# Attention scores from residual rows times query-weighted keys, two heads at once

## The chip, the cores and the metric

The kernel runs on one core of a Trainium2 chip. A core has a TensorE (PE), which multiplies a stationary 128x128 operand by up to 512 moving columns into one PSUM bank, a VectorE (DVE), a ScalarE (ACT), a GpSimd (POOL) and a SyncE (SP), each with its own queue of instructions that it works through in order, and 16 DMA engines that they share. Here SP issues the loads and POOL the stores. The metric is the device time of one execution in microseconds; lower is better.

## The reference

One layer of a streaming encoder on 512 rows of 2048 numbers: four mixers behind one input projection, cross-attention into 256 memory rows with 4 heads of 512, and a feed-forward block, each between two RMS norms. What matters here is the attention, where `h` is the normed residual row and `m` the normed memory:

```python
def memory_cross_attention(h, m, wq, wkv, wo):
    q = (h @ wq).reshape(bsz, T, XA_HEADS, XA_HEAD_DIM)
    k, v = jnp.split(m @ wkv, 2, axis=-1)
    ...
    s = jnp.einsum('bthd,bmhd->bhtm', q, k).astype(jnp.float32) * XA_HEAD_DIM ** -0.5
    p = jax.nn.softmax(s, axis=-1).astype(v.dtype)
    o = jnp.einsum('bhtm,bmhd->bthd', p, v).reshape(bsz, T, D_MODEL)
    return o @ wo
```

All of it is in float32. The output is the residual stream after the three sub-layers.

## The kernel before

**Products.** A float32 operand is split into a high part (rounded to float32r) and a low part, the rest; `split` (L155) makes the high part on ACT and the low part on DVE. `mul3` (L176) adds three products of such parts into a PSUM bank, high by high (L177), high by low (L178) and low by high (L179), so each 128-deep step costs three matmuls. `weights` (L164) loads 256 rows by 512 columns of a weight matrix (512 KB) on SP into `raw` and splits them into `whi` and `wlo`; with `gain` it multiplies each row by a norm's gain on the way (two splits of 512 columns instead of one of 1024). The three names have three buffers each (`wp`). Products go to five PSUM banks called `mm` or three called `ps`.

**Stages around the change.** In phase 1 the keys of each head (`k_d`) and later its values (`v_d`) are computed from the memory and written to DRAM, split. The end of phase 1 is the output projection of the mixers (`y_proj`, with `w_out`), four passes of 512 columns. Behind the last pass `advance` takes each of four blocks of 128 rows through the norm and the residual sum (`ad_x`), transposes the new rows on PE (L231, four banks a block), and splits them into `act`, which holds the residual rows transposed. It also makes the next norm's factor `r2a`; that factor is not multiplied into `act` but into the scores.

In the same stretch `value_out` (L880) runs for heads 0 to 2: it multiplies a head's values by that head's rows of `xa_wo` and writes the product (`vw_d`) to DRAM, 24 matmuls of 512 columns for each of four column passes. Each needs nothing of `advance`, so its matmuls stand between the transposes of `advance` in PE's order.

Phase 2 is a loop over the four heads. `proj_a` multiplies the head's 512 columns of `xa_wq` (with the gain of norm 2) by `act` into four `mm` banks, which are split into `qh` and `ql`. `attention` (L851) loads the head's keys (`at_kh`, `at_kl`) and computes for each block of 128 rows the scores against 256 memory rows in a `ps` bank, then the maximum, the exponential with its row sum, and the division (`at_p`). The probabilities are transposed on PE and split into `pth`, `ptl`, two heads in one pair of tiles. Behind head 0 stands `value_out` for head 3. Then `y_proj` multiplies the probabilities of all heads by `vw_d`.

A scheduler sets the order of each engine's queue from the order of the program and from the buffers; a tile that is asked for while all its buffers are in use makes the instruction that first writes it wait.

## Time and profile before

| What | Value |
|---|---|
| Median of the runs, lowest to highest | 2770.33 us, 2769.64 to 2773.34 |
| The profiled execution's own time | 2771.02 us |
| Its span in the trace | 2769.1 us |
| Granted TensorE clock | 0.989 |
| DMA, mean over the span | 155 GB/s |
| HBM read, written | 351.30 MB, 74.47 MB |
| Loads of `xa_wq` issued | 1077.8 to 1273.5 us, 32 of 512 KB |
| Loads of `xa_wo` issued | 978.7 to 1145.7 us, 32 of 512 KB |

The span is cut into 40 equal slices below; each digit is the busy share of a slice in tenths, 9 meaning 90% or more. A slice is 69.2 us, so the stages above lie in slices 15 to 19 (1003 us is at 14.5 slices, 1308 us at 18.9).

```profile
PE   8999999999999999999979999999999998999997
DVE  5735557446662355434589989888888989999966
ACT  5623423233552245423455545444444445665542
DMA  8732322344675258532654434343333326577656
```

A busy share is a mean over stages with different limits, and matmuls overlap, so the prediction reads stages and starts of instructions.

### The profile page before, as it was taken

The numbers are of one execution on the slowest core, as the hardware profiler recorded it, in microseconds if no ns is written. First come the engines' busy times: TensorE is split into PE (matmuls) and PEld (weight loads), VectorE is DVE, ScalarE is ACT, GpSimd is POOL, SyncE is SP. The second block draws the span as 40 slices with busy tenths as digits, with TensorE's granted clock in tenths as the row PEclk, the third lists the DMA queues.
The fourth block names the chain that finished last, engine by engine and source line by source line (L and its number), as shares of the span: only waits on it lengthen the run. The fifth ranks groups of instructions, "written<-read, shape, count | busy, mean of one in ns | idle before, by whom it ended". The sixth has DMA issues, their size and how long they took to land. (4 is left out here: it accounts for less than half of the span.)

```text
span 2769.1 us, 35279 instructions
## 1 busy us (share of the span) xinstructions
PE 2680.7 (97%) x13426; PEld 2249.7 (81%) x13426; DVE 1942.7 (70%) x2869; ACT 1261.1 (46%) x1918; POOL 139.5 (5%) x219
## 2 busy tenths in 40 slices
PE   8999999999999999999979999999999998999997
PEld 6788788878778877888857888888888887888875
DVE  5735557446662355434589989888888989999966
ACT  5623423233552245423455545444444445665542
POOL 0000000100000001000000000000000000000002
PEclk9999999999999999999989999999999999999998
DMA  8732322344675258532654434343333326577656
GB/s 287 237 105 86 96 69 80 109 130 125 216 256 215 93 188 307 174 100 88 213 185 144 141 118 127 114 130 116 124 122 120 121 103 245 196 198 192 166 125 225
DMA packets 158755, 428.08 MB, mean 155 GB/s; under 512 B 18157, under 2 KB 29306, under 8 KB 147706
## 3 DMA queue, kind: packets, MB, share of 16 engines
q1 hardware_dynamic: 140154, 355.57, 39.2%
q0 software_dynamic: 18432, 70.27, 8.8%
q8 instruction: 105, 1.72, 0.3%
q14 instruction: 64, 0.52, 0.1%
HBM read 351.30 MB, written 74.47 MB: 154 GB/s over the span
## 5 line engine op out<-in xcount | busy, mean ns | idle before, releaser
L162 DVE SCALAR_TENSOR_TENSOR wlo<-raw,PA,whi 128x512 fp32r<-128x512 f32 x368 | 263.1, 747 | 298.7 <-ACT whi L161 298.6
L161 ACT ACTIVATE whi<-raw,PA 128x512 fp32r<-128x512 f32 x368 | 247.8, 718 | 398.0 <-PE mm L178 211.0
L1088 PE MATMUL mm<-L,whi 128*128 128x512 f32 x1448 | 367.8, 396 | 15.7 <-ACT f_x L1111 8.6
L177 PE MATMUL mm<-act,whi 128*128 128x512 f32 x832 | 329.8, 396 | 0.0
L179 PE MATMUL mm<-act,wlo 128*128 128x512 f32 x832 | 326.7, 393 | 0.0
L178 PE MATMUL mm<-act,whi 128*128 128x512 f32 x832 | 326.1, 392 | 0.0
L1088 PEld LDWEIGHTS mm<-L,whi 128*128 128x128 f32 x1448 | 263.4, 191 | 65.0 <-ACT f_x L1111 9.6
L991 ACT CAST whi<-raw 128x1024 fp32r<-128x1024 f32 x176 | 184.9, 1051 | 237.3 <-PE ps L1088 77.3
L177 PE MATMUL mm<-whi,act 128*128 128x512 f32 x640 | 251.6, 394 | 4.2 <-ACT act L158 3.7
L1088 PE MATMUL ps<-L,whi 128*128 128x512 f32 x1016 | 254.8, 392 | 0.0
L178 PE MATMUL mm<-wlo,act 128*128 128x512 f32 x640 | 250.8, 392 | 2.4 <-DVE wlo L162 2.4
L179 PE MATMUL mm<-whi,act 128*128 128x512 f32 x640 | 250.0, 392 | 0.2 <-DVE act L159 0.2
L159 DVE TENSOR_TENSOR wlo<-raw,whi 128x1024 fp32r<-128x1024 f32 x92 | 112.4, 1224 | 191.7 <-ACT whi L158 191.3
L992 DVE TENSOR_TENSOR wlo<-raw,whi 128x1024 fp32r<-128x1024 f32 x176 | 214.0, 1217 | 5.1 <-ACT whi L991 5.1
L1091 PEld LDWEIGHTS mm<-L,wlo 128*128 128x128 f32 x1448 | 198.0, 191 | 18.2 <-DVE wlo L992 4.2
L1088 PEld LDWEIGHTS ps<-L,whi 128*128 128x128 f32 x1016 | 182.6, 189 | 32.6
L1091 PE MATMUL mm<-L,wlo 128*128 128x256 f32 x1448 | 203.3, 283 | 2.7 <-DVE wlo L992 2.7
L991 ACT CAST whi<-sum 128x1024 fp32r<-128x1024 f32 x132 | 137.6, 1045 | 129.3 <-DVE wlo L992 64.6
L992 DVE TENSOR_TENSOR wlo<-sum,whi 128x1024 fp32r<-128x1024 f32 x132 | 161.6, 1224 | 43.4 <-ACT whi L991 42.5
L179 PEld LDWEIGHTS mm<-act,wlo 128*128 128x128 f32 x832 | 156.3, 188 | 32.3 <-issue 0.5
L158 ACT CAST whi<-raw 128x1024 fp32r<-128x1024 f32 x92 | 96.8, 1054 | 186.9 <-PE mm L179 137.6
L178 PEld LDWEIGHTS mm<-act,whi 128*128 128x128 f32 x832 | 156.4, 188 | 30.8 <-issue 0.7
(505 smaller groups left out, 4908.7 us busy)
## 6 DMA issues: line engine op xcount, KB each, us to landing
raw<-in_w_gu_dram SPq DMA_DIRECT2D x186, 512.0 KB, 3.6
raw<-in_w_in_dram SPq DMA_DIRECT2D x88, 512.0 KB, 3.7
rawB<-in_w_down_dram SPq DMA_DIRECT2D x40, 1024.0 KB, 5.0
raw<-in_xa_wkv_dram SPq DMA_DIRECT2D x64, 512.0 KB, 4.4
raw<-in_w_out_dram SPq DMA_DIRECT2D x32, 512.0 KB, 3.9
raw<-in_xa_wo_dram SPq DMA_DIRECT2D x32, 512.0 KB, 6.6
raw<-in_xa_wq_dram SPq DMA_DIRECT2D x32, 512.0 KB, 4.0
raw<-vw_d SPq DMA_DIRECT2D x28, 512.0 KB, 4.2
```

What stands on the lines that cost most here:

```text
L158: nc.scalar.copy(hi, src)
L159: nc.vector.tensor_tensor(lo, src, hi.bitcast(F32), op=ALU.subtract)
L161: nc.scalar.activation(hi, src, AF.Copy, scale=scale)
L162: nc.vector.scalar_tensor_tensor(lo, src, scale, hi.bitcast(F32), op0=ALU.mult, op1=ALU.subtract)
L177: nc.tensor.matmul(o, ah, bh, start=start, stop=False, skip_group_check=reopen)
L178: nc.tensor.matmul(o, ah, bl, start=False, stop=False, skip_group_check=reopen)
L179: nc.tensor.matmul(o, al, bh, start=False, stop=stop, skip_group_check=reopen)
L991: nc.scalar.copy(hl[0], src)
L992: nc.vector.tensor_tensor(hl[1], src, hl[0].bitcast(F32), op=ALU.subtract)
L1088: nc.tensor.matmul(bank, wh[:, k], t[k].rearrange("p s n -> p (s n)"), start=k == 0 and m in (1, 2, 5), stop=k == 7, **kw)
L1091: nc.tensor.matmul(bank[:, 0:256], wl[:, k], t[k][:, 0], start=False, stop=k == 7, **kw)
```

## The change

For each head the query weights are first multiplied by the keys: `g = wq[:, head] @ k[head].T`, 2048 by 256. The scores are then the residual rows times `g`, so the queries themselves are no longer made. The new function `key_query` makes `g` for all four heads, in the place in phase 1 where `value_out` for heads 0 to 2 stood, ahead of those. It reads the transposed query weights (`xa_wqt`, transposed on the host as other weights are laid out there), multiplies by the gain of norm 2 while it splits the product, and writes both parts to DRAM (`g_d`, two heads side by side, 16 MB in all). `attention` now takes a pair of heads: for each of 16 k-steps it multiplies the rows' `act` by 512 columns of `g`, which come from DRAM straight into buffers called `whi` and `wlo`, into four `mm` banks, one for each block of rows. Softmax and transposes are as before, for two heads together. `value_out` for head 3 now stands behind both pairs.

In `key_query` a product's bank has high weights by both key parts in its 512 columns, and low weights by the high keys added to the first 256; the two halves are then added (copy on ACT, add on DVE) and split. The buffers that `g` is split into (`at_vh`, `at_vl`) are those that `value_out` loads values into, two of each.

```diff
+    g_d = dr.tile([2, 2, P, KT, 2 * MEM], F32, name="g_d")
...
+            for h in range(XH):
+                key_query(h, pl)
             for h in range(3):
                 value_out(h, pl, 2)
...
+    def key_query(h, pl):
+        kk = pl.tile([P, 4, 2, MEM], F32R, name="kq_k")
+        for i in range(2):
+            nc.sync.dma_start(kk[:, :, i].bitcast(F32), k_d[h][i].rearrange("p (d m) -> p d m", d=4))
+        for q in range(4):
+            w = [weights(xa_wqt, h * XHD + dc * 2 * P, q * 512) for dc in range(2)]
+            gh, gl = (pl.tile([P, 4 * MEM], F32R, name="at_v" + i, bufs=2).rearrange("p (k m) -> p k m", k=4)
+                      for i in "hl")
+            for j in range(4):
+                js = slice(j * P, (j + 1) * P)
+                o = mm.tile([P, 512], F32, name="mm")
+                for d in range(4):
+                    wh, wl = w[d // 2]
+                    nc.tensor.matmul(o, wh[:, d % 2, js], kk[:, d].rearrange("p s m -> p (s m)"), start=d == 0,
+                                     stop=d == 3, skip_group_check=True)
+                for d in range(4):
+                    nc.tensor.matmul(o[:, 0:MEM], w[d // 2][1][:, d % 2, js], kk[:, d, 0], start=False,
+                                     stop=d == 3, skip_group_check=True)
+                g = pl.tile([P, MEM], F32, name="kq_g", bufs=2)
+                nc.scalar.copy(g, o[:, MEM:])
+                nc.vector.tensor_tensor(g, o[:, 0:MEM], g, op=ALU.add)
+                split(gh[:, j], gl[:, j], g, gcol(2, q * 4 + j))
+            for i, src in enumerate((gh, gl)):
+                nc.gpsimd.dma_start(g_d[h // 2, i, :, 4 * q:4 * q + 4, h % 2 * MEM:(h % 2 + 1) * MEM], src.bitcast(F32))
...
-    def attention(h, qh, ql, pl, ph, pl_):
+    def attention(act, p, pl, ph, pl_):
...
+        o = [mm.tile([P, 512], F32, name="mm") for _ in range(NT)]
+        lhs = act_lhs(act)
+        for kc in range(KT // 2):
+            g = [wp.tile([P, 2, 512], F32R, name=n) for n in ("whi", "wlo")]
+            for i in range(2):
+                nc.sync.dma_start(g[i].bitcast(F32), g_d[p, i, :, 2 * kc:2 * kc + 2])
+            for t in range(NT):
+                for kk in range(2):
+                    k = kc * 2 + kk
+                    ah, al = lhs(k, t)
+                    mul3(o[t], ah, al, g[0][:, kk], g[1][:, kk], k == 0, k == KT - 1)
...
-                for h in range(XH):
-                    qh = pl.tile([P, 4, T], F32R, name="at_qh", bufs=2)
-                    ql = pl.tile([P, 4, T], F32R, name="at_ql", bufs=2)
-                    proj_a(act, xa_wq, h * XHD, lambda j, o: split(qh[:, j], ql[:, j], o), 2)
-                    ks = slice(2 * (h % 2), 2 * (h % 2) + 2)
-                    attention(h, qh, ql, pl, pt[h // 2][0][:, ks], pt[h // 2][1][:, ks])
-                    if h == 0:
-                        value_out(3, pl)
+                for p in range(2):
+                    attention(act, p, pl, *pt[p])
+                value_out(3, pl)
```

Three places in the engines' order show what stands where. First PE beside the transposes of the second row block of `advance` (`ad_x`), before; `mm` are banks, `at_vh` the values of `value_out`:

```order
L177 MATMUL mm_8269<-whi_8272,at_vh_8176 128x512
L231 MATMUL ps_7983<-C_83,ad_x_7963 128x128 x4
L231 MATMUL ps_7991<-C_83,ad_x_7963 128x128 x4
L178 MATMUL mm_8269<-wlo_8273,at_vh_8176 128x512
L231 MATMUL ps_7999<-C_83,ad_x_7963 128x128 x4
```

And the same place now:

```order
L870 MATMUL mm_8380<-kq_k_8177,whi_8326 128x512
L233 MATMUL ps_7984<-C_83,ad_x_7964 128x128 x4
L870 MATMUL mm_8380<-kq_k_8177,whi_8326 128x512
L233 MATMUL ps_7992<-C_83,ad_x_7964 128x128 x4
L233 MATMUL ps_8000<-C_83,ad_x_7964 128x128 x4
L870 MATMUL mm_8380<-kq_k_8177,whi_8332 128x512 x2
L873 MATMUL mm_8380<-kq_k_8177,wlo_8327 128x256 x2
```

`value_out` has gone from between the transposes, and `key_query` has taken its place; up to the last transpose of `advance` there were 142 matmuls of the one, and there are 178 of the other.

Second, SP's queue where the keys of head 2 are loaded, with what each row waits for (a semaphore of PE, of DVE, or of an earlier DMA):

```order
L168 DMA raw_8834<-in_xa_wqt_dram 128x2x512 [waits DMAHW3_49,DMAHW0_49,DVE_49]
L168 DMA raw_8840<-in_xa_wqt_dram 128x2x512 [waits DMAHW1_49,DVE_49]
L860 DMA kq_k_8759<-k_d2_91 128x4x256 [waits PE_49]
L860 DMA kq_k_8759<-k_d2_91 128x4x256
L168 DMA raw_8906<-in_xa_wqt_dram 128x2x512 [waits DMAHW2_49,DVE_49]
L168 DMA raw_8912<-in_xa_wqt_dram 128x2x512 [waits DMAHW3_49,DVE_49]
```

These loads are new; the first of the two waits for PE, and the weight loads behind it for their turn. Further down the same queue, where `value_out` of head 0 begins (`xa_wo` are its weights):

```order
L168 DMA raw_9391<-in_xa_wo_dram 128x2x512 [waits DMAHW7_49,DMAHW4_49,DVE_49]
L168 DMA raw_9409<-in_xa_wo_dram 128x2x512 [waits DMAHW5_49,DMAHW0_49,DVE_49]
L168 DMA raw_9435<-in_xa_wo_dram 128x2x512 [waits DMAHW6_49,DVE_49]
L923 DMA at_vh_9341<-v_d0_93 128x1024 [waits DMASW4_49,DMASW5_49,DMASW2_49,DMASW0_49]
L923 DMA at_vl_9342<-v_d0_93 128x1024 [waits DMASW5_49,DMASW6_49,DMASW3_49,DMASW1_49]
```

Before, the values of heads 0 and 1 were loaded ahead of the output projection; now head 0's follow five of the weight loads, and wait for stores of POOL (DMASW).

Third, DVE in the middle of `key_query` (`kq_g` the product that is added up, `at_vl` its low part, `wlo` the low part of the next weights):

```order
L877 TENSOR_TENSOR kq_g_8885<-mm_8876,kq_g_8885 128x256
L877 TENSOR_TENSOR kq_g_8899<-mm_8890,kq_g_8899 128x256
L161 TENSOR_TENSOR wlo_8981<-raw_8978,whi_8980 128x1024
L164 SCALAR_TENSOR_TENSOR at_vl_8847<-kq_g_8885,PA_84,at_vh_8846 128x256
L164 SCALAR_TENSOR_TENSOR at_vl_8847<-kq_g_8899,PA_84,at_vh_8846 128x256
```

The banks go in pairs, with a split of weights between the steps of a pair; in `value_out` DVE had the split of weights alone.

More of the change, by code (lines that the diff above doesn't have):

```diff
@@ L71, in build @@
           gdn_dt_bias, gdn_norm_g, ssm_conv_w, ssm_conv_b, ssm_A_log, ssm_dt_bias, ssm_D,
-          ssm_norm_g, w_out, xa_wq, xa_wkv, xa_wo, w_gu, w_down, w_last, cst, out, dbg=None,
+          ssm_norm_g, w_out, xa_wqt, xa_wkv, xa_wo, w_gu, w_down, w_last, cst, out, dbg=None,
           phases=(1, 2, 3)):
@@ L94, in build @@
     x, mem = x[0], mem[0]
-    w_in, w_out, xa_wq, xa_wkv, xa_wo = w_in[0], w_out[0], xa_wq[0], xa_wkv[0], xa_wo[0]
+    w_in, w_out, xa_wkv, xa_wo = w_in[0], w_out[0], xa_wkv[0], xa_wo[0]
     pool_w = pool_w[0]
@@ L848, in v_load @@
         return mt
-    def attention(h, qh, ql, pl, ph, pl_):
-        hl = [pl.tile([P, 1024], F32R, name="at_k" + s, bufs=2) for s in "hl"]
-        for s in range(2):
-            nc.sync.dma_start(hl[s].bitcast(F32), k_d[h][s])
-        kh, kl = (a.rearrange("p (d m) -> p d m", d=4) for a in hl)
+    def key_query(h, pl):
[23 more added lines that the diff above has]
+    def attention(act, p, pl, ph, pl_):
         sc = float(XHD) ** -0.5
-        pr = pl.tile([P, NT, MEM], F32, name="at_p")
         rs = sm.tile([P, 2 * NT], F32, name="at_rs")
@@ L861, in attention @@
         nc.vector.tensor_scalar(rs[:, NT:], r2a, -sc, None, op0=ALU.mult)
-        for t in range(NT):
-            ts_ = slice(t * P, (t + 1) * P)
-            s = ps.tile([P, 512], F32, name="ps")[:, :MEM]
-            for d in range(4):
-                mul3(s, qh[:, d, ts_], ql[:, d, ts_], kh[:, d], kl[:, d], d == 0, d == 3)
-            mx = sm.tile([P, 1], F32, name="at_mx")
-            nc.vector.tensor_reduce(mx, s, axis=AX.X, op=ALU.max)
-            nc.vector.tensor_tensor(mx, mx, rs[:, NT + t:NT + t + 1], op=ALU.mult)
-            sum_ = sm.tile([P, 1], F32, name="at_s")
-            nc.scalar.activation(pr[:, t], s, AF.Exp, bias=mx, scale=rs[:, t:t + 1], accum_out=sum_)
+        o = [mm.tile([P, 512], F32, name="mm") for _ in range(NT)]
[9 more added lines that the diff above has]
+                    mul3(o[t], ah, al, g[0][:, kk], g[1][:, kk], k == 0, k == KT - 1)
+        pr = pl.tile([P, NT, 512], F32, name="at_p", bufs=2)
+        for t in range(NT):
+            mx = sm.tile([P, 2], F32, name="at_mx")
+            nc.vector.tensor_reduce(mx, o[t].rearrange("p (h m) -> p h m", h=2), axis=AX.X, op=ALU.max)
+            nc.vector.tensor_scalar(mx, mx, rs[:, NT + t:NT + t + 1], None, op0=ALU.mult)
+            sum_ = sm.tile([P, 2], F32, name="at_s")
+            for i in range(2):
+                ms = slice(i * MEM, (i + 1) * MEM)
+                nc.scalar.activation(pr[:, t, ms], o[t][:, ms], AF.Exp, bias=mx[:, i:i + 1], scale=rs[:, t:t + 1],
+                                     accum_out=sum_[:, i:i + 1])
             nc.vector.reciprocal(sum_, sum_)
-            nc.vector.tensor_scalar(pr[:, t], pr[:, t], sum_, None, op0=ALU.mult)
-        for m in range(2):
+            for i in range(2):
+                ms = slice(i * MEM, (i + 1) * MEM)
+                nc.vector.tensor_scalar(pr[:, t, ms], pr[:, t, ms], sum_[:, i:i + 1], None, op0=ALU.mult)
+        for m in range(4):
             tp = ps.tile([P, T], F32, name="ps")
@@ L1356 @@
         'gdn_dt_bias', 'gdn_norm_g', 'ssm_conv_w', 'ssm_conv_b', 'ssm_A_log', 'ssm_dt_bias', 'ssm_D',
-        'ssm_norm_g', 'w_out', 'xa_wq', 'xa_wkv', 'xa_wo', 'w_gu', 'w_down', 'w_last', 'cst']
+        'ssm_norm_g', 'w_out', 'xa_wqt', 'xa_wkv', 'xa_wo', 'w_gu', 'w_down', 'w_last', 'cst']
 _OUTS = [((1, T, D), 'float32')]
@@ L1364, in laid_out @@
     a['cst'] = constants()
+    a['xa_wqt'] = np.ascontiguousarray(np.asarray(inputs['xa_wq'])[0].T)
     w = np.asarray(inputs['ffn_w_gu'])[0].reshape(2, 8, P, 2, HT, P)
```

## The prediction

> **What bounds the kernel now.** I began with the page's first part, to see which engine is full:
>
> ```profile
> PE 2680.7 (97%) x13426; PEld 2249.7 (81%) x13426; DVE 1942.7 (70%) x2869; ACT 1261.1 (46%) x1918; POOL 139.5 (5%) x219
> ```
>
> TensorE is busy 97% of the span, so a change of matmul counts should show in the time. But a busy share says nothing about one stage, so I asked for the windows of the stages that the change touches: from the end of the first output projection to the last row transposes of `advance` (1003 to 1054 us), the rest of `value_out` for heads 0 to 2 (to 1085), and attention with head 3's `value_out` (to 1308.4). Columns: the window, its length, then busy time of PE, weight loads, DVE, ACT and POOL, TensorE's clock, DMA share, GB/s.
>
> ```profile
> 1003.00:1054.00 51.00, 44.95 (x220) 36.08 (x219) 43.40 (x128) 33.76 (x49) 8.04 (x15) 0.97 0.84 304
> 1054.00:1085.00 31.00, 30.19 (x131) 24.08 (x130) 15.09 (x31) 15.93 (x22) 5.00 (x10) 1.00 0.83 271
> 1085.00:1308.40 223.40, 223.40 (x1076) 187.08 (x1075) 85.13 (x149) 79.61 (x133) 6.33 (x12) 1.00 0.43 140
> sum 305.40, PE 298.54 PEld 247.25 DVE 143.62 ACT 129.29 POOL 19.37; mean PE 99.51 PEld 82.42 DVE 47.87 ACT 43.10 POOL 6.46
> ```
>
> The third window is pure TensorE: no gap, DVE and ACT under 40%, DMA at 0.43. In the first, TensorE already has gaps, DVE is busy 43.4 of 51 us and DMA 0.84. **The change moves work out of the third window, where only TensorE is scarce, into the first, where everything is scarce.** All else stays, so the sum is for these 305.4 us.
>
> Next, the price of one matmul. Matmuls overlap, so I read the timeline of starts, not durations:
>
> ```profile
> 1125.72 0.39 PE L179 MATMUL mm<-act,wlo 128*128 128x512 f32 x1
> ...
> 1129.80 0.39 PE L179 MATMUL mm<-act,wlo 128*128 128x512 f32 x1
> 1130.03 0.28 PE L177 MATMUL ps<-at_kh,at_qh 128*128 128x256 f32 x1
> ...
> 1131.34 0.28 PE L179 MATMUL ps<-at_kh,at_ql 128*128 128x256 f32 x1
> ```
>
> 18 steps in 4.08 us: 0.2267 us for 512 columns. 11 steps in 1.31 us: 0.119 us for 256.
>
> **The change, part by part. Tensor work.** Removed: the query projection, 4 heads x 16 k x 4 columns x 3 = 768 at 0.2267 = 174.1 us, and the scores, 4 x 4 x 4 x 3 = 192 at 0.119 = 22.9; together 197.0. Added: `key_query`, 64 banks x (4 of 512 + 4 of 256 columns) = 256 x 0.2267 + 256 x 0.119 = 88.5, and the new scores, 2 pairs x 16 k x 4 row blocks x 3 = 384 x 0.2267 = 87.1; together 175.6. Were every stage like the third window, the gain would be **21.4 us**. The 32 transposes of the probabilities stay.
>
> **The third window after.** 223.4 - 197.0 + 87.1 = 113.5 us. The weights of these scores come by DMA as they are: two 512 KB loads per 24 matmuls (5.44 us), 193 GB/s, under the 304 of the first window; buffers are three deep, so I cost them at nothing. The softmax of a pair is behind its last matmuls: a reduction and two exponentials of
>
> ```profile
> L868 DVE TENSOR_REDUCE at_mx<-ps 128x1 f32<-128x256 f32 x16 | 6.6, 422 | 3.3 <-PE ps L179 3.1
> L871 ACT ACTIVATE at_p<-ps,at_mx,at_rs 128x256 f32<-128x256 f32 x16 | 9.0, 563 | 14.8 <-DVE at_mx L869 14.8
> ```
>
> 0.56 us each and two scalings, some 3 us. The new order puts matmuls of the fifth bank, and then of `value_out`, between the transposes; I take 1.5 us for each of the two pairs (ends 0 and 3): 116.5.
>
> **`value_out` of heads 0 to 2**, now after all of `key_query`: 288 x 0.2267 = 65.3, its own cover unchanged.
>
> **First stage: `key_query` beside `advance`.** Per block of four banks it asks TensorE for 5.53 us. Its price on DVE, by issue distance:
>
> ```profile
> 1600.61 1.22 DVE L992 TENSOR_TENSOR wlo<-sum,whi 128x1024 fp32r<-128x1024 f32 x1 [0.34 <-ACT whi L991]
> 1601.75 0.42 DVE L1166 TENSOR_TENSOR f_t<-mm,f_t 128x256 f32<-128x256 f32 x1
> 1602.09 1.21 DVE L1037 TENSOR_TENSOR sum<-sum,raw 128x1024 f32<-128x1024 f32 x1
> 1603.22 0.42 DVE L1168 SCALAR_TENSOR_TENSOR f_t<-f_t,f_t 128x256 f32<-128x256 f32 x1
> ```
>
> 1.13 us for a weight's low part, 0.34 for a 256-column add from a bank. The scaled subtraction has a column as its scalar; by
>
> ```profile
> L162 DVE SCALAR_TENSOR_TENSOR wlo<-raw,PA,whi x368: 706/746/754, 8.4 to 1289.0; 128x512 fp32r<-128x512 f32 x184
> L162 DVE SCALAR_TENSOR_TENSOR act<-ps,PB,act x16: 339/346/353, 727.4 to 789.0; 128x128 fp32r<-128x128 f32 x16
> ```
>
> 256 columns take about 0.48 us, 0.40 by issue. A block: 2 x 1.13 + 4 x 0.74 = 5.2 us of DVE if it never waits. But copy (ACT), add (DVE), scaled copy (ACT) and subtraction (DVE) hand over four times per bank with two `kq_g` buffers:
>
> ```profile
> L1165 ACT COPY f_t<-mm 128x256 f32<-128x256 f32 x44 | 16.1, 366 | 10.3 <-PE mm L1091 10.3
> L158 ACT CAST whi<-raw 128x1024 fp32r<-128x1024 f32 x92 | 96.8, 1054 | 186.9 <-PE mm L179 137.6
> ```
>
> With 0.37, 0.42, 0.48 and 0.48 the chain of a pair of banks, overlapped as the order has it, is about 1.9 us; with one weight split beside it 2.9 or so: **5.9 us a block**. Ends: 5.5 (TensorE alone) and 8.1 (the four steps one after the other, 7.0, and a 1.05 us cast).
>
> The steps of `advance` itself, and where the stage ended before (the last of its transposes on PE):
>
> ```profile
> 1020.28 2.74 DVE L765 SCALAR_TENSOR_TENSOR ad_x<-y,rs_r,ad_x 128x512 f32<-128x512 f32 x4
> 1024.01 1.89 DVE L159 TENSOR_TENSOR act<-ps,act 128x512 fp32r<-128x512 f32 x3 [0.99 <-ACT act L158]
> ...
> 1028.53 0.16 DVE L151 TENSOR_TENSOR rsq_t<-nr_r 128x1 f32<-128x1 f32 x1
> 1028.60 0.15 DVE L151 TENSOR_TENSOR rsq_t<-rs_r 128x1 f32<-128x1 f32 x1
> 1028.72 0.16 DVE L152 SCALAR_TENSOR_TENSOR rsq_t<-rsq_t,mr_v 128x1 f32<-128x1 f32 x1
> ```
>
> ```profile
> 1051.19 0.65 PE L231 MATMUL ps<-C,ad_x 128*128 128x128 f32 x4
> ```
>
> Until those transposes the new order has 178 of the 512 `key_query` matmuls. DVE must issue in that time 19 adds (6.5 us), 18 subtractions (7.2), 10 low parts (11.3), 16 row updates at 0.67 (10.7), 16 splits at 0.60 (9.6) and some 80 small steps at 0.09 (7.3): 53 us. The same count before (12 low parts, 13.6, no adds or subtractions, two evictions, 1.2) gives 42.4 in 51.0 us, so 8.6 of waits; with them and 3 more for the new hand-overs **65 us** (ends 53 and 77). TensorE needs 42 of these, so DVE is the bound here.
>
> **The rest of `key_query`: new waits.** `kq_k` has one buffer, so head h+1's keys can be loaded only after head h's last matmul; SP holds that load and the weight loads queued behind it, and TensorE, in order, waits for both halves. What such a pair of 512 KB loads takes:
>
> ```profile
> raw<-in_xa_wq_dram SPq DMA_DIRECT2D x32, 512.0 KB, 4.0
> raw<-in_xa_wo_dram SPq DMA_DIRECT2D x32, 512.0 KB, 6.6
> at_vh<-v_d SPq DMA_DIRECT2D x4, 512.0 KB, 8.9
> at_kh<-k_d SPq DMA_DIRECT2D x4, 512.0 KB, 10.4
> ```
>
> 4.0 with free engines, 10.4 in a burst. The new blocks move 2.1 MB in under 6 us, so the engines are near full: I take 6.5. And a wait of that kind has an aftermath:
>
> ```profile
> 1021.13 1.89 PE L231 MATMUL ps<-C,ad_x 128*128 128x128 f32 x8 [2.90 <-issue]
> 1022.67 0.77 PE L178 MATMUL mm<-wlo,at_vh 128*128 128x512 f32 x1
> ...
> 1024.52 0.45 PE L177 MATMUL mm<-whi,at_vh 128*128 128x512 f32 x1
> ```
>
> After 2.9 us idle matmuls last 0.77 us, not 0.39, until 1024.5, some 1.5 us lost. So 8 us for a head change (ends 4 and 12). The first of the three falls into the stage that DVE bounds anyway (42 + 8 < 65): nothing. Left are 334 matmuls: the rest of head 1, 2.44 blocks x 5.9 = 14.4; heads 2 and 3, each 22.1 + 8, in whose pause DVE and ACT catch up: 60.2. **74.6 us** (ends 58 + 2 x 4 = 66, and 10.4 x 8.1 + 24 = 108).
>
> The Trainium skill, "DMA: Bandwidth & Descriptors", section "Anatomy of one DMA", fits one transfer (for the other issuing path) as about 2.0 us plus bytes over 436e3 per us; a 1.05 MB pair would be 4.4 us by it, an estimate, and the sum 4.2 us shorter. The 8.9 and 10.4 rows speak against it here.
>
> **From `key_query` to `value_out`.** The values used to be loaded far ahead, head 0's at 854.0 us:
>
> ```profile
> L884 SPq DMA_DIRECT2D at_vh<-v_d x4: 442/463/477, 854.0 to 1097.3; - x4
> ```
>
> Now they take the buffers (`at_v`) that the last blocks write to DRAM from, and stand on SP behind five weight loads, the last of which waits for a split that waits for the last block. So they are issued about when TensorE runs dry: the 8.9 us row, **9 us** (ends 4 and 12).
>
> **Sum.** 65 + 74.6 + 9 + 65.3 + 116.5 = 330.4, against 305.4: **25.0 us more**. The profiled execution took 2771.0 us (span 2769.1), 0.7 over the median 2770.3, so 2796.0 there and 2795 as a median. With all ends low 53 + 66 + 4 + 65.3 + 113.5 = 302, 4 us faster; with all high 77 + 108 + 12 + 65.3 + 119.5 = 382, 76 slower.
>
> **Rivals.**
> 1. *The pauses vanish under the evictions* (faster). If the keys land while ACT and DVE still drain the five banks and the split weights, TensorE's pauses cost nothing of their own and DVE's issue time alone counts: 55 + 60.5 + 4 + 65.3 + 113.5 = 298, **2763**. It decides if a pair of key loads lands within some 4 us (five banks at 0.74). For it: the 4.0 us row. Against: 6.6, 8.9 and 10.4. Chance 0.08.
> 2. *Pauses half as long and good overlap*: 57 + 66 + 5 + 65.3 + 114.5 = 308, **2773**, no change to speak of. Chance 0.09.
> 3. *The transfers are the bound*: the two stages move 46 MB (16.8 of weights, 16.8 written, 4.2 of keys, 8.4 of `advance`). At the busiest stretch of before,
>
> ```profile
> 1020.00:1040.00 20.00, 16.54 (x81) 13.52 (x81) 16.36 (x45) 12.65 (x19) 4.29 (x8) 0.91 0.93 334
> 1040.00:1060.00 20.00, 19.33 (x95) 15.70 (x94) 18.37 (x63) 14.42 (x21) 3.22 (x6) 1.00 0.96 352
> ```
>
> that is 131 to 138 us, less than my 140; but the three pauses also hold SP's weight loads, and if these gaps cannot be filled it is 135 + 24 = 159: **2815**. Chance 0.13.
> 4. *The hand-overs do not overlap*: 8.1 us a block. 77 + 10.4 x 8.1 + 16 + 9 + 65.3 + 116.5 = 368, **2833**. For it: two `kq_g` buffers, and splits of weights that stand between the steps. Against: the order issues them in pairs. Chance 0.12.
>
> **How the numbers follow.** My forecast, 2795 with a range of its own of 2779 to 2812, gets 0.58. About 0.2% (5.5 us) is what a measurement can tell from no change. Faster is rival 1, 0.08; within 0.2% rival 2, 0.09; slower the rest, 0.83. The range that leaves out rival 1 and most of rival 4 is 2771 to 2828.
>
> **What would show it.** Right: PE gaps of 5 to 10 us at each change of `kq_k` and before the first `at_vh` matmul, put down to those DMAs; DVE over 85% busy until the last `ad_x` transposes, and these 12 to 16 us later than at 1051; from the first new score on no gap over 2 us and about 192 matmuls in 44 us. Wrong: gaps under 3 us at the head changes (rivals 1, 2); DMA share at 0.95 with PE waiting for `raw` (rival 3); ACT and DVE waiting for each other through all 16 blocks at 8 us (rival 4). A slower clock over the whole kernel, or a loss outside these stages, would make all of it wrong.

## The result and the profile after

The changed kernel takes 2822.4 us (median of 4 runs, 2820.3 to 2823.8), the kernel before 2771.7 beside it: ratio 1.0185, 95% interval 1.0173 to 1.0197. The forecast was 2795: slower, as measured, but the loss is 51 us and not 25. 2822 lies outside the forecast's own range, 2779 to 2812, and inside the wider one, 2771 to 2828.

The page's first part, after: TensorE has 64 matmuls fewer and is busy as long as before, in a span 50.9 us longer.

```profile
PE 2680.5 (95%) x13362; PEld 2246.1 (80%) x13362; DVE 1970.3 (70%) x2921; ACT 1293.2 (46%) x1998; POOL 164.1 (6%) x251
```

From here on "the stretch" is the time from the end of the output projection to the first matmul on the probabilities `pth`: 305.0 us before, 357.7 after in the profiled runs. Outside it little moved: ahead of it 1003.5 us before and 1001.2 after, behind it 1460.6 and 1461.1. The windows of the changed kernel, cut at the prediction's stages (columns as there): to the last row transposes; the rest of head 1; pause, head 2; pause, head 3; the hand-over; `value_out` 0 to 2; a gap; attention with `value_out` 3.

```profile
1001.00:1062.90 61.90, 45.77 (x242) 37.56 (x241) 49.67 (x157) 39.79 (x72) 8.22 (x12) 0.86 0.70 247
1062.90:1085.00 22.10, 16.09 (x81) 13.20 (x79) 18.25 (x48) 14.86 (x28) 4.17 (x6) 0.92 0.83 278
1085.00:1093.00 8.00, 0.00 (x0) 0.01 (x1) 5.30 (x9) 3.90 (x9) 1.85 (x3) 0.66 1.02 327
1093.00:1119.30 26.30, 25.34 (x128) 20.97 (x128) 16.80 (x30) 16.25 (x31) 3.60 (x5) 0.91 0.71 248
1119.30:1127.80 8.50, 0.00 (x0) 0.01 (x1) 5.70 (x10) 4.21 (x10) 2.41 (x4) 0.64 1.02 348
1127.80:1153.50 25.70, 25.03 (x128) 20.73 (x128) 16.80 (x30) 16.19 (x31) 3.55 (x5) 0.92 0.72 251
1153.50:1162.70 9.20, 0.01 (x1) 0.03 (x1) 5.70 (x10) 4.26 (x10) 2.46 (x4) 0.62 0.97 303
1162.70:1237.80 75.10, 69.93 (x288) 56.27 (x288) 25.43 (x21) 33.75 (x43) 11.95 (x22) 0.93 0.83 270
1237.80:1242.40 4.60, 0.16 (x1) 0.00 (x0) 0.00 (x0) 0.00 (x0) 0.00 (x0) 0.86 1.00 361
1242.40:1358.90 116.50, 116.09 (x513) 94.55 (x514) 29.50 (x58) 28.12 (x58) 4.34 (x8) 0.98 0.63 217
```

Four windows hold no matmul but for a stray record, and in each the DMA share is 0.97 or more: TensorE stands while transfers are under way. Who it waited for in this stretch (total, times, longest):

```profile
PE mm L870 <- DMA kq_k<-k_d: 23.0, 3, 8.6
PE mm L179 <- DMA at_vh<-v_d: 9.2, 1, 9.2
PE mm L873 <- DVE wlo L161: 6.8, 3, 4.8
PE mm L870 <- DVE kq_g L877: 4.9, 4, 3.1
PE mm L179 <- DMA whi<-g_d: 4.5, 1, 4.5
```

Each pause has a tail. The timeline of TensorE behind the last of them, where the scores begin:

```profile
1242.42 2.48 PE L179 MATMUL mm<-whi,act 128*128 128x512 f32 x4 [4.45 <-DMA whi<-g_d]
1244.69 0.63 PE L180 MATMUL mm<-wlo,act 128*128 128x512 f32 x1
1245.12 0.63 PE L181 MATMUL mm<-whi,act 128*128 128x512 f32 x1
...
1247.25 0.63 PE L181 MATMUL mm<-whi,act 128*128 128x512 f32 x1
1247.68 0.52 PE L179 MATMUL mm<-whi,act 128*128 128x512 f32 x1
1248.03 0.40 PE L180 MATMUL mm<-wlo,act 128*128 128x512 f32 x1
```

Starts are 0.43 us apart until 1247.7, then 0.23: for 5.3 us after 4.45 us of idleness matmuls go at half rate, some 2.4 us lost. All this against the forecast:

| Stage | Forecast us | Measured us |
|---|---|---|
| to the last `ad_x` transposes | 65 | 61.9 |
| rest of head 1 | 14.4 | 22.1 |
| heads 2 and 3 with their pauses | 60.2 | 68.5 |
| hand-over to `value_out` | 9 | 9.2 |
| `value_out` 0 to 2 | 65.3 | 75.1 |
| first load of `g` | 0 | 4.6 |
| attention and `value_out` 3 | 116.5 | 116.5 |
| sum | 330.4 | 357.9 |

### The profile page after: what moved, and what is told of

Its sections match the earlier page's. It is cut to its first block, busy times and chain, and to the rows that moved or that the text cites. A ratio compares the mean times of both kernels' runs of the same rounds, so it can differ in the third digit from the quotient of the medians.

```text
span 2820.0 us, 35497 instructions
## 1 busy us (share of the span) xinstructions
PE 2680.5 (95%) x13362; PEld 2246.1 (80%) x13362; DVE 1970.3 (70%) x2921; ACT 1293.2 (46%) x1998; POOL 164.1 (6%) x251
## 5 line engine op out<-in xcount | busy, mean ns | idle before, releaser
L164 DVE SCALAR_TENSOR_TENSOR wlo<-raw,PA,whi 128x512 fp32r<-128x512 f32 x304 | 218.0, 748 | 198.7 <-ACT whi L163 198.6
L163 ACT ACTIVATE whi<-raw,PA 128x512 fp32r<-128x512 f32 x304 | 205.4, 720 | 306.5 <-PE mm L180 145.1
L161 DVE TENSOR_TENSOR wlo<-raw,whi 128x1024 fp32r<-128x1024 f32 x124 | 151.2, 1224 | 252.5 <-ACT whi L160 252.4
L179 PE MATMUL mm<-whi,act 128*128 128x512 f32 x768 | 303.1, 396 | 6.6 <-DMA whi<-g_d 4.5
L180 PE MATMUL mm<-wlo,act 128*128 128x512 f32 x768 | 301.5, 393 | 1.8 <-DVE wlo L164 1.8
L181 PE MATMUL mm<-whi,act 128*128 128x512 f32 x768 | 300.8, 393 | 0.2 <-DVE act L161 0.2
L1025 ACT CAST whi<-raw 128x1024 fp32r<-128x1024 f32 x176 | 185.1, 1052 | 237.4 <-PE mm L1122 70.5
L160 ACT CAST whi<-raw 128x1024 fp32r<-128x1024 f32 x124 | 130.4, 1053 | 231.9 <-PE mm L181 183.9
L179 PE MATMUL mm<-act,whi 128*128 128x512 f32 x576 | 230.4, 400 | 0.0
L181 PE MATMUL mm<-act,wlo 128*128 128x512 f32 x576 | 227.7, 395 | 0.0
L180 PE MATMUL mm<-act,whi 128*128 128x512 f32 x576 | 227.0, 394 | 0.0
L1026 DVE TENSOR_TENSOR wlo<-raw,whi 128x1024 fp32r<-128x1024 f32 x176 | 214.3, 1218 | 5.3 <-ACT whi L1025 5.3
L179 PEld LDWEIGHTS mm<-whi,act 128*128 128x128 f32 x768 | 145.2, 189 | 39.2 <-DMA whi<-g_d 4.9
L180 PEld LDWEIGHTS mm<-wlo,act 128*128 128x128 f32 x768 | 145.2, 189 | 32.6 <-DVE wlo L164 3.0
```

The source lines that it names most:

```text
L160: nc.scalar.copy(hi, src)
L161: nc.vector.tensor_tensor(lo, src, hi.bitcast(F32), op=ALU.subtract)
L163: nc.scalar.activation(hi, src, AF.Copy, scale=scale)
L164: nc.vector.scalar_tensor_tensor(lo, src, scale, hi.bitcast(F32), op0=ALU.mult, op1=ALU.subtract)
L179: nc.tensor.matmul(o, ah, bh, start=start, stop=False, skip_group_check=reopen)
L180: nc.tensor.matmul(o, ah, bl, start=False, stop=False, skip_group_check=reopen)
```

## The experiments

**Theory.** The loss is TensorE's waits for loads that cannot be issued before the last reader of their only buffer is done, each with its tail at half clock, and the hand-overs between ACT and DVE. **Rival.** The transfers bind in any order: the change moves 34 MB more (the profiles count 428.1 MB before and 461.7 after). The medians, with the ratio to the kernel before, and the stretch of each profiled run:

| Run | Median us | Ratio, 95% interval | Stretch us |
|---|---|---|---|
| changed kernel | 2822.4 | 1.0185, 1.0173 to 1.0197 | 357.7 |
| changed_again | 2826.9 | 1.0196, 1.0181 to 1.0211 | 363.1 |
| swap | 2830.4 | 1.0213, 1.0198 to 1.0229 | 361.1 |
| two_k | 2813.5 | 1.0150, 1.0135 to 1.0165 | 347.0 |
| own_v | 2818.2 | 1.0168, 1.0147 to 1.0188 | 350.1 |
| two_k_own_v | 2806.4 | 1.0126, 1.0110 to 1.0143 | 339.9 |
| eight_e | 2798.7 | 1.0098, 1.0079 to 1.0117 | 331.7 |
| eight_e_own_g | 2805.8 | 1.0124, 1.0105 to 1.0142 | 344.4 |
| half_stores | 2790.2 | 1.0070, 1.0049 to 1.0091 | 326.5 |
| long_runs | 2798.4 | 1.0098, 1.0081 to 1.0116 | 335.0 |
| four_kq_g | 2791.6 | 1.0072, 1.0056 to 1.0088 | 325.9 |
| vo3_back | 2829.2 | 1.0210, 1.0194 to 1.0226 | 356.0 |
| values_first | 2781.8 | 1.0039, 1.0026 to 1.0052 | 313.0 |
| values_first_half | 2768.2 | 0.9993, 0.9984 to 1.0002 | 305.8 |
| four_raw | 2782.7 | 1.0039, 1.0026 to 1.0052 | 314.7 |
| interleaved | 2798.5 | 1.0094, 1.0079 to 1.0109 | 333.7 |
| interleaved_2 | 2788.5 | 1.0068, 1.0054 to 1.0082 | 322.9 |
| interleaved_3 | 2790.4 | 1.0077, 1.0064 to 1.0090 | 323.5 |

**How far these numbers carry.** Two runs settle it: the changed kernel itself again, and one part undone.

> The changed kernel once more, nothing edited. If the 7 us by which the control and vo3_back were slower come from the edits, this is 2822 again, with the output projection ending at 1001 us. If they come from what differs between one set of runs and the next, ahead of the stretch, this can come out as far as 2829, with a later end of the output projection and the same 358 us from there to the first matmul on the probabilities.

It ran from 2820.2 to 2832.9, with a stretch of 363.1 us and the end of the output projection at 1005.4 instead of 1001.2. Two edits further down that leave the work as it is, vo3_back and swap, gave medians of 2829.2 and 2830.4 and stretches of 356.0 and 361.1. So a difference of up to 8 us between two medians, or 7 us between two single stretches, shows nothing by itself, and I lean on waits that come or go and on differences above that.

```diff
-                for p in range(2):
-                    attention(act, p, pl, *pt[p])
-                value_out(3, pl)
+                attention(act, 0, pl, *pt[0])
+                value_out(3, pl)
+                attention(act, 1, pl, *pt[1])
```

> One part of the change undone: value_out of head 3 stands between the two pairs again, all else as in the changed kernel. The forecast had 116.5 us for attention and value_out 3, and this stretch took that. So no part of the loss should lie here: 2822 within 4 us. Rival (the new place of value_out 3 costs: its weights hold up the next stage, or the softmax of pair 0 was covered better): 3 us or more below 2822.

Measured 2829.2, but a stretch of 356.0: the 7 us are inside the spread of the changed kernel itself. No loss shows in the new place of `value_out` 3.

**Buffers for keys and values.** The pools of this stage leave 2 KB of SBUF, too little for a second `kq_k`. So the pool of `y` was put on top and closed after head 1; first alone, as a control:

```diff
-            yp = pool("yp", stack=s1)
             pl = pool("adp", stack=s1)
+            syp = ExitStack()
+            yp = pool("yp", stack=syp)
...
-            for h in range(XH):
+            for h in range(2):
+                key_query(h, pl)
+            syp.close()
+            for h in range(2, XH):
                 key_query(h, pl)
```

> Control for the next three: the pool of y is put above that of advance and closed after head 1 of key_query, so that its 41 KB can be used again; nothing else is edited, but the loads of ad_x for the next stage may now start earlier. Theory (each loss is a load that must wait for the last reader of its one buffer): the same time as the changed kernel, 2822 within 4 us, the three kq_k waits of 6.4, 8.1 and 8.6 us and the at_vh wait of 9.2 us all still there. Rival (the transfers are the bound): the 2 MB of ad_x that come earlier lengthen the stretch by about 6 us, 2828.

2830.4, stretch 361.1, inside the spread; all four waits are still there (23.7 us in three for `kq_k`, 9.3 for `at_vh`). The 8 us above 2822 are near what the rival had forecast for the early `ad_x`, but the unchanged kernel reached 2833 as well, so neither is decided. Then with a second `kq_k`:

```diff
+            kp = pool("kqp", stack=s1)
             for h in range(2, XH):
-                key_query(h, pl)
+                key_query(h, pl, kp if h == 2 else pl)
...
-        kk = pl.tile([P, 4, 2, MEM], F32R, name="kq_k")
+        kk = kp.tile([P, 4, 2, MEM], F32R, name="kq_k")
```

> As the control, with a second kq_k buffer for head 2, so that the keys of heads 2 and 3 load while the head before still computes; head 1's pause is left. Theory: the waits for kq_k of 8.06 and 8.58 us go, and with each some 2 us of matmuls at half the clock: 20 us less than the control, about 2802; the at_vh wait stays at 9. Rival 1 (transfers are the bound): the waits move to wlo or raw and the time falls by less than 8 us, above 2814. Rival 2 (ACT and DVE need the pauses to catch up): waits for kq_g and wlo grow in heads 2 and 3 to some 4 us each and the gain is about 12, 2810.

17 us less than the control in the median, 14 in the stretch (the control is at the upper end of the spread: against the eight runs of the changed kernel, whose median is 2823.4, this gain and the next two are 7 us smaller). TensorE's waits in it:

```profile
PE mm L179 <- DMA at_vh<-v_d: 8.2, 1, 8.2
PE mm L875 <- DVE kq_g L882: 8.2, 8, 3.5
PE mm L878 <- DVE wlo L161: 7.4, 8, 4.9
PE mm L875 <- DMA kq_k<-k_d: 7.1, 1, 7.1
```

Two of three waits for `kq_k` are gone. The gain lies between theory and rival 2: in the control `kq_g` cost 6.1 and `wlo` at that place 5.9 us, so some of the time comes back as hand-overs. The values' side alone (blocks of `g` of heads 2 and 3 in buffers of the new pool, one `kq_k`):

```diff
-            gh, gl = (pl.tile([P, 4 * MEM], F32R, name="at_v" + i, bufs=2).rearrange(
+            gh, gl = (vp.tile([P, 4 * MEM], F32R, name="at_v" + i, bufs=2).rearrange(
```

> As the control, with one kq_k, but blocks of g of heads 2 and 3 in buffers of their own, so that value_out's loads of at_v no longer wait for stores of g. Theory: the 9.2 us before the first at_vh matmul and the 2.1 us for at_vl go, and the 2 us at half the clock behind them: 12 to 13 us less than the control, about 2809; the kq_k waits stay. Rival (transfers are the bound): the values, loaded in key_query, lengthen the kq_k waits by as much as is won: 2818 or more.

12 us less than the control, 11 in the stretch, and no wait for `at_vh` or `at_vl` is left, as the theory said; the vanished waits, 9.3 and 1.3 us, are the firmer sign. Both together:

> Both edits: second kq_k, and own buffers for the blocks of g of heads 2 and 3. Theory: the gains add up, 20 + 13 = 33 us less than the control, about 2789, with the clock at 1.00 from the start of head 2 to the end of value_out 2 but for the stop of 2.3 us there. Rival (transfers are the bound): with no pauses left the stretch of heads 2 and 3 runs at a DMA share of 0.95 or more with waits for raw and wlo, and the sum of the two gains is cut by a third or more, above 2800.

24 us less, 21 in the stretch: not the 33, and somewhat less than the two measured gains added up, 29 and 25. Two windows of `key_query` without pauses:

```profile
1080.00:1098.00 18.00, 16.20 (x82) 13.68 (x81) 12.88 (x24) 11.21 (x23) 4.51 (x6) 0.91 1.00 352
1098.00:1116.00 18.00, 14.85 (x75) 11.78 (x74) 13.96 (x27) 12.14 (x25) 3.22 (x5) 0.97 1.02 387
```

TensorE is busy 31 of 36 us and the DMA engines all the time: the rival's picture, though only once the pauses are gone. But `key_query` behind the last transposes took 80.1 us here and 78.9 in two_k, so no more was lost in it than there. What is new is that ACT stood in `value_out`; its timeline, and SP's beside it:

```profile
1163.42 1.05 ACT L160 CAST whi<-raw 128x1024 fp32r<-128x1024 f32 x1
1172.20 1.04 ACT L160 CAST whi<-raw 128x1024 fp32r<-128x1024 f32 x1 [7.73 <-DMA raw<-in_xa_wo_dram]
```

```profile
1160.89 0.34 SPq L981 DMA_DIRECT2D ad_x<-x_d  x1
1161.33 4.79 SPq L168 DMA_DIRECT2D raw<-in_xa_wo_dram  x3
1166.17 0.74 SPq L981 DMA_DIRECT2D ad_x<-x_d  x1
```

The next stage's 1 MB loads of `ad_x` found the freed memory and went between `value_out`'s weights, where the two runs before had them at 1062 to 1068 us, beside `key_query`. TensorE stopped 4.7 us for `whi` there and then ran at half rate for some 5 us: together about what is missing from the sum of the two gains. That `ad_x` held the weights is read from the order, not tested alone.

**`value_out`'s stores and the first load of `g`.** In the changed kernel ACT, which casts the weights, also copies to `at_e`:

```profile
1199.59 0.59 ACT L928 COPY at_e<-mm 128x512 f32<-128x512 f32 x1 [5.47 <-DMA vw_d<-at_e]
...
1201.31 1.99 ACT L160 CAST whi<-raw 128x1024 fp32r<-128x1024 f32 x2
```

A store for which ACT waits 5.5 us holds the next casts, and TensorE stops 2.3 us for `whi` until 1202.4. Eight `at_e` in the freed memory, which also keeps `ad_x` out of it:

```diff
-                e = pl.tile([P, 512], F32, name="at_e", bufs=2)
+                e = (ep or pl).tile([P, 512], F32, name="at_e", bufs=8 if ep else 2)
```

> As two_k_own_v, with eight buffers at_e (for value_out of heads 0 to 2) in the pool that was freed; the next stage's ad_x, which in the last run came early and held the weights (ACT waited 7.7 us for raw at 1172 us, TensorE 4.7 for whi), then finds no free space and loads late again. Theory of waits: that stop with its 2 us at half the clock and the waits behind vw_d's stores (some 3 us) go: value_out 0 to 2 in about 68 us instead of 76, 2797 in all. Rival (transfers are the bound): the bytes are the same, so no more than 2 us less than 2806.

2798.7 and a stretch 8 us shorter, near the 2797 that the theory gave. ACT's waits for these stores are gone and `ad_x` loads at 1234 us; `value_out` took 71.3 us, not 68, while ACT waited 24.4 us for weights (17.3 before). The run doesn't tell `ad_x` and `at_e` apart. Next, `g` in buffers of its own:

```diff
-            g = [wp.tile([P, 2, 512], F32R, name=n) for n in ("whi", "wlo")]
+            g = [pl.tile([P, 2, 512], F32R, name="at_g" + n, bufs=4) for n in "hl"]
```

> As eight_e, and attention takes g into four buffers of its own instead of whi and wlo, which value_out's last weights still hold. Theory: the gap of some 4 us before the first score and the half clock behind it go, 5 to 6 us less than eight_e. Rival (SP's order decides): the loads of g stand on SP behind the last raw anyway and the gap stays, 1 us or less.

Neither: 7 us more, and a gap of 14.2 us before the first score. SP waited 7.8 us for TensorE's last `value_out` matmul before the first load of `at_gh`, most likely because the attention's pool lies in memory that `value_out` still used. The cost of the first load thus stays a reading of the trace, not an experiment.

**What bounds `key_query` then.** In eight_e, ACT waited in the stretch of `key_query` behind advance for

```profile
ACT kq_g L881 <- DVE at_vl L164: 10.1, 11, 1.5
ACT whi L160 <- DMA raw<-in_xa_wqt_dram: 8.2, 4, 3.3
```

that is for a subtraction to free one of two `kq_g`, and for weights to land. Three runs on it: fewer bytes, longer runs per store, more `kq_g`.

```diff
-            for i, src in enumerate((gh, gl)):
+            for i, src in enumerate((gh,)):
...
-                nc.sync.dma_start(g[i].bitcast(F32), g_d[p, i, :, 2 * kc:2 * kc + 2])
+                nc.sync.dma_start(g[i].bitcast(F32), g_d[p, 0, :, 2 * kc:2 * kc + 2])
```

> As eight_e, but the low parts of g are not stored and the scores use the high parts in their place (8.4 of 16.8 MB of stores left out, all loads kept). It measures what bounds key_query once its pauses are gone: in two_k_own_v its 334 matmuls from the last row transposes on took 81 us, 7.7 us a block of four banks where TensorE needs 5.5. Theory 1 (transfers): some 25 MB move in that stretch at 0.97 DMA share; 5.5 MB less is about 16 us less, and a few us less beside advance: 15 to 20 us below eight_e. Theory 2 (hand-overs between ACT and DVE, and raw freed only by DVE): under 5 us less.

8.5 us less in the median, 5.2 in the stretch: between the two and nearer to the hand-overs, but at the limit of what can be told.

```diff
-    g_d = dr.tile([2, 2, P, KT, 2 * MEM], F32, name="g_d")
+    g_d = dr.tile([2, 2, 2, P, KT, MEM], F32, name="g_d")
```

> As eight_e, with g_d laid out head by head: a store writes 4 KB in one run per partition instead of four of 1 KB, and a load of the scores is two DMAs with runs of 2 KB instead of one with 4 KB. If the length of the runs costs DMA time in the stores, the 754 ns of a store's issue fall towards the 540 ns of vw_d's, the transfers get shorter and key_query gains 5 to 10 us. If only bytes count: within 2 us of eight_e, and attention's g loads (193 GB/s needed) still hidden.

2798.4, no gain, though a store's issue on POOL did get shorter; the rows of eight_e and then of long_runs (min/median/max ns):

```profile
L885 POOL DMA_DIRECT2D g_d<-at_vh x16: 752/752/764, 1017.3 to 1154.2; - x16
```

```profile
L885 POOL DMA_DIRECT2D g_d<-at_vh x16: 531/531/537, 1016.0 to 1155.6; - x16
```

```diff
-                g = pl.tile([P, MEM], F32, name="kq_g", bufs=2)
+                g = pl.tile([P, MEM], F32, name="kq_g", bufs=4)
```

> As eight_e, with four buffers kq_g instead of two. Half the stores gave 8.5 us, not 15 to 20, so the theory is now that hand-overs between ACT and DVE bound key_query: ACT waited 10.1 us for a subtraction to free a kq_g, and TensorE 8.2 us for an add to free a bank. Theory 1 (two kq_g): copies and adds of the next pair go ahead of the subtractions, the 8.2 us go, a block takes 6.4 us instead of 7.3 and the whole is 8 to 10 us below eight_e. Theory 2 (the weights' splits and the transfers set the pace together): the waits move to whi, wlo and raw, 3 us or less.

7 us less in the median, 6 in the stretch, by themselves inside the spread. TensorE's waits in `key_query` behind advance are now

```profile
PE mm L875 <- ACT whi L160: 7.8, 7, 2.4
PE mm L878 <- DVE wlo L161: 1.6, 2, 1.0
```

The waits for `kq_g` went there, 8.2 us before; those for the weights' high parts grew, which ACT makes when `raw` has landed.

**The place beside advance.** `value_out` 0 to 2 first, as before the change, then all of `key_query` (two `kq_k`, own `g` blocks, four `kq_g`):

```diff
+            for h in range(3):
+                vs = values(h, pl, 2)
+                for c in range(4):
+                    value_out(h, c, vs, pl)
+            syp.close()
+            kp = pool("kqp", stack=s1)
             for h in range(XH):
-                key_query(h, pl)
-            for h in range(3):
-                value_out(h, pl, 2)
+                kk = keys(h, kp)
+                for q in range(4):
+                    key_query(h, q, kk, kp)
```

> value_out of heads 0 to 2 stands beside advance again, as before the change, and all of key_query behind it, with two kq_k, own buffers for g and four kq_g in the memory of y; attention as in the changed kernel. It asks what the place beside advance costs. Theory (key_query's DVE work cannot be hidden beside advance): the stage to value_out 2 takes the 82 us of before; key_query's 16 blocks some 6.6 us each, 106; a pause of about 4 for its first keys; attention 120: 312, so about 2778. Rival (the place does not matter, hand-overs and transfers take the same total wherever they stand): as four_kq_g, 2789 or more.

Stretch 313.0 for a forecast of 312, 13 us under four_kq_g. The fastest of those that compute everything, and still slower than before. The total fits the forecast by parts that do not: advance with `value_out` took 85.2 us (82), `key_query` 112.8 (106), its first keys no pause (4), attention 115 (120). Nor does the run show that the place itself costs. It has two `kq_k` for every head, while four_kq_g still has, beside advance,

```profile
PE mm L875 <- DMA kq_k<-k_d: 8.3, 1, 8.3
```

This stop and its tail account for the gain up to the first score: `key_query`, advance and `value_out` together took 206.5 us there and 198.0 here. Most of the rest is the first load of `g`, for which TensorE waits 3.2 us there and not here. As far as these two runs show, what the place costs is the room for a second `kq_k`, which is there only once `y` is gone. The windows of `key_query` in values_first, and one of ACT's waits there:

```profile
1090.20:1146.00 55.80, 48.18 (x259) 38.51 (x258) 41.69 (x78) 38.93 (x80) 11.62 (x16) 1.00 0.84 302
1146.00:1203.00 57.00, 47.36 (x256) 37.97 (x255) 42.86 (x81) 37.92 (x80) 11.68 (x16) 1.00 0.92 322
```

```profile
ACT whi L160 <- DMA raw<-in_xa_wqt_dram: 22.3, 15, 3.0
```

16 blocks in 112.8 us, 7.05 each, with the clock at 1.00 and no stop above 2.3 us. Transfers, splits, or the lead of the loads? The first by leaving out the low stores again, as in half_stores; the last with a fourth buffer for weights:

> As values_first, but the low parts of g are not stored and the scores use the high parts in their place (8.4 of 16.8 MB of stores left out, loads kept). In values_first key_query took 112.8 us for 16 blocks, TensorE waited 12.1 us for whi and 4.4 for wlo, and ACT 22.3 us for raw to land. Theory 1 (now the transfers bound it, at some 312 GB/s): a quarter less bytes takes a block to about 5.9 us, 17 us less than values_first, 2765. Theory 2 (the four splits of a weight and of a bank per block on ACT and DVE): a block stays above 6.7 us and the gain is 6 us or less, 2776 or more.

13.6 us less in the median, 7.2 in the stretch (in the profiled runs another 4.5 lie ahead of it, where the two kernels are the same); `key_query` took 105.0 us, 6.6 a block, and ACT's wait for `raw` fell to 12.3. A quarter of the bytes is worth a third of the 1.5 us by which a block misses TensorE's pace: the transfers are a part, not the whole.

```diff
+        raw = rp.tile([P, 2, 512], F32, name="kq_w") if rp else wp.tile([P, 2, 512], F32, name="raw")
...
+        w = [weights(xa_wqt, h * XHD + dc * 2 * P, q * 512, None, kp if dc and q % 2 else None) for dc in range(2)]
```

> As values_first, but every fourth weight tile of key_query is loaded into a buffer of its own, so that four instead of three loads can be under way. In values_first SP waited some 80 us in key_query for a split to free raw, and ACT then 22 us for raw to land. Theory 1 (the lead of the loads): TensorE's 12.1 us of waits for whi fall below 5, key_query takes 103 us instead of 113 and the stretch 303 to 306 instead of 313. Theory 2 (bandwidth): the loads land later as they are more, the stretch stays within 3 us of 313.

Stretch 314.7, `key_query` 112.1: no gain, as theory 2 has it. TensorE waited five times for `whi` and not ten, but 12.0 us as before, 6.0 of them at once, in a burst of loads (DMA share 1.03 from 1128 to 1137 us). A longer lead is not the remedy; that bandwidth alone sets the pace is not shown by it.

**Can it be faster than before?** If transfers and hand-overs are what binds, `key_query`'s blocks belong beside matmuls that need less of both:

```diff
+                for q in range(4):
+                    key_query(h, q, kk, kp)
+                    value_out(h + 1, q, vs, pl)
...
+                attention(act, 0, pl, *pt[0], lambda i: key_query(2 + i // 4, i % 4, kk[i // 4], pl, ps, "ps"))
```

> As values_first, but each block of key_query of heads 0 and 1 alternates with a column block of value_out 1 and 2, those of heads 2 and 3 with the score matmuls of the first pair (in the three ps banks), and value_out 3 with those of the second pair. TensorE then has 11 us of work for each block's chain of hand-overs, and about 290 GB/s are needed instead of 340. Theory (losses are waits beside which TensorE had no other work): the stretch takes the 284 us of pure matmul time plus 6 for advance and 5 to 10 for the first keys and the softmax: 295 to 300, 2760 to 2765, faster than before the change. Rival (the weights' three buffers, now shared by loads of g and splits, become the bound, or the 41 MB more of transfers cost wherever they stand): 312 or more, 2778 and up.

2798.5: with only `value_out` 0 as cover TensorE stood idle for 13.5 of 20 us beside advance (1040 to 1060), 7.0 of them in a wait for the first keys. A second order with more cover there, and a third with a later start in phase 2:

> As values_first, but value_out 0 and 1 alone stand beside advance, value_out 2 and 3 alternate by column block with key_query of heads 0 and 1, and key_query of heads 2 and 3 alternates with the score matmuls of the first pair from the second step on, every second g in a buffer of its own. In the first interleaved run the alternating blocks of key_query and value_out ran at TensorE's pace (95 per cent busy); lost were some 20 us beside advance, where only value_out 0 was left as cover, 12 for keys and 10 for g in the shared buffers. Theory (these three were the loss): the stretch takes 60 + 88 + 88 + 45 us and some 10 of waits, 291 to 300, and the whole 2757 to 2766. Rival (the loads of g, the weights and the stores get into each other's way in any order): no better than values_first, 2780 or more.

> As interleaved_2, but key_query of heads 2 and 3 begins only at the fourth step of the first pair's scores (three blocks then stand behind them and cover the softmax), their keys are asked for at the first and fifth step, and the second pair takes g into the weights' buffers alone. Theory (the loss left was the pause for keys of 8.8 us and the 4.6 and 3.3 us for g): 12 to 17 us less than interleaved_2, 2772 to 2777, level with the kernel before within half a per cent. Rival (the transfers of keys, g and weights at the beginning of phase 2 take the same time in any order): 6 us less or fewer, 2782 or more.

Both missed, at 2788.5 and 2790.4. The idea holds where it runs; two windows of interleaved_2 in the alternating part of phase 2:

```profile
1204.00:1224.00 20.00, 20.00 (x104) 17.05 (x103) 11.20 (x20) 9.84 (x20) 2.25 (x3) 1.00 0.81 292
1224.00:1244.00 20.00, 20.00 (x104) 17.03 (x103) 9.33 (x18) 9.88 (x19) 2.25 (x3) 1.00 0.86 298
```

TensorE never stops, at nearly the traffic of values_first, so about 295 GB/s alone do not hold it up. But phase 2 begins with a pause of 8.8 us for keys in interleaved_2 and 10.6 in interleaved_3. SP's timeline of the latter:

```profile
1163.16 13.20 SPq L168 DMA_DIRECT2D raw<-in_xa_wqt_dram  x2
1176.66 1.20 SPq L872 DMA_DIRECT2D kq_k<-k_d  x2
```

The scheduler put weight loads ahead of the keys, and SP held these for 13 us. An order in which the keys go first was not tried.

## Why the prediction was right in direction and wrong in size

The stages came to 27.5 us more than the forecast's sum: 16.0 in the rest of `key_query`, 9.8 in `value_out` and 4.6 at the first load of `g`, less 3.1 in the first stage.

- **Tensor work.** Right. That attention with `value_out` 3 took the forecast 116.5 us to the tenth is luck: 3 us were put down for the softmax, which cost one wait of 0.3, and some 2.4 us went on the slow clock behind the first load of `g`.
- **First stage.** 65 forecast, 61.9 measured. The last transposes came at 1062.5, 11 us later than before (12 to 16 forecast), but DVE was busy 80% of the window, not over 85: TensorE also stood 6.4 us for the first keys, which were put at nothing, and 4.8 for a weight's low part. The 51.0 us of before from which the waits were worked out end 2 us behind the last transposes, which are done at 1051.9.
- **The failed step: "the rest of `key_query`", 74.6 us.** It took 90.6. The rest of head 1 was priced as steady blocks of 5.9 us, 14.4; it took 22.1. TensorE alone needs 13.5 of these; it stood 6.0 us and lost about 1.4 at half rate. 1.4 of the waits are for a step of advance on ACT and 1.3 for a weight's low part; the longest, 3.1, goes back to a weight that landed late, as the bank's copy and add stand behind that weight's splits:

```profile
1075.04 1.05 ACT L160 CAST whi<-raw 128x1024 fp32r<-128x1024 f32 x1 [2.54 <-DMA raw<-in_xa_wqt_dram]
1075.99 0.64 ACT L876 COPY kq_g<-mm 128x256 f32<-128x256 f32 x2
1076.12 1.23 DVE L161 TENSOR_TENSOR wlo<-raw,whi 128x1024 fp32r<-128x1024 f32 x1 [1.75 <-ACT whi L160]
1077.26 0.75 DVE L877 TENSOR_TENSOR kq_g<-mm,kq_g 128x256 f32<-128x256 f32 x2
1077.82 2.05 PE L870 MATMUL mm<-kq_k,whi 128*128 128x512 f32 x4 [3.11 <-DVE kq_g L877]
```

  No experiment isolates this part. Heads 2 and 3 were priced at TensorE's 22.1 us and 8 for a pause with its slow clock, 60.2 in all; they took 68.5. The pauses were 8.1 and 8.6 without the slow clock, which cost 2.0 to 2.3 more. Behind it, that ACT and DVE would have caught up was nearly right: banks follow each other in 1.40 us, 5.6 a block, and the last bank waits 0.9 and 0.7 us for `kq_g`.
- **"Its own cover unchanged", 65.3 us for `value_out`.** It took 75.1. It was not unchanged: `value_out` now starts at half clock, waits 2.1 us for `at_vl` behind a store, and stops 2.3 and 0.8 us for a weight whose split stands behind two `at_e` that wait for their stores (ACT waited 20.2 us for these in all). own_v and eight_e took the waits for stores away.
- **"I cost them at nothing", the loads of `g`.** True for all but the first, which stands behind `value_out`'s weights: 4.6 us and a slow start. For this only the trace speaks.
- **The hand-over.** 9 forecast, 9.2 measured, and this too is luck. The forecast was one load of 8.9 us, issued about when TensorE runs dry, at 1153.5. The trace has the load 4.7 us later:

```profile
1158.23 0.34 SPq L923 DMA_DIRECT2D at_vh<-v_d  x1
```

  It waited for a store of `g` that was issued at 1153.0, and then landed in 4.5 us, half the row's 8.9.
- **The key loads.** The Trainium skill's fit ("DMA: Bandwidth & Descriptors", "Anatomy of one DMA") gives an estimate of 4.4 us for a pair; the trace does not agree: TensorE stood 6.4 to 8.6 us for each, and each of the eight loads of keys took 6.4 to 7.3 us from issue to landing.
- **Rivals.** 1 and 2 fell with the pauses. 4 fell: blocks ran at 5.6 us in heads 2 and 3. 3 was wrong for this kernel (a DMA share of 0.71 between the pauses) but is part of what is left without them. That 2815 and 2833, the times of rivals 3 and 4, lie nearer to 2822 than 2795 does is no support for either.

Not settled: why that weight landed late in the rest of head 1; what holds `key_query` at 7.05 us a block in values_first beyond the share of the transfers; and whether an order exists that is faster than before.

## What to carry to other kernels

A stage that loads a whole operand into a single buffer costs TensorE the load's time in a busy queue, here 6 to 9 us, and some 2 us of half clock behind it; count both, at every turn. When work is moved next to a stage, every buffer that it shares (keys, values, evictions, weights) is a wait to be priced, and so is the memory that a second buffer would need. A saving in matmuls that is bought with DRAM traffic has to be set against that traffic: here 21 us of matmuls against 34 MB. When a term of a sum comes out right, look whether its parts did: two of these did not.

## What the hardware showed unexpectedly

- After 4.45 us of idleness TensorE ran at half rate for 5.3 us. The Trainium skill ("TensorE: Matmul & The Clock Gate", "What's actually happening") has the clock full again after at least one busy window of about 3.4 us, a window that runs freely; the half rate agrees with the trace, the 5.3 us here are longer than one such window.
- A GpSimd store issues in 752 ns with runs of 1 KB and in 531 ns with runs of 4 KB, and neither the transfers nor the kernel got shorter by it.
- The changed kernel spread over 2820 to 2833 us in eight runs, and in its two profiled ones the output projection ended at 1001 and 1005 us; the kernel before stayed within 2766 and 2776.
